# Value differences of a stick-breaking attention spread over a projection and four head pairs, and each pair's output split issued after the next pair's turned weights

## The chip, the cores and the metric

The kernel runs on one core of one Trainium2 chip. A core has TensorE (PE, with its weight loads shown as PEld), VectorE (DVE), ScalarE (ACT), GpSimd (POOL) and SyncE (SP), each with its own queue of instructions that it works off in order. Transfers are requested from a queue (here SP's and GpSimd's) and carried out beside the engines. The metric is the device time of the whole program in microseconds; lower is better. Three runs of the kernel before took 1161.62, 1164.15 and 1165.39 us, the median is 1164.15 us.

## The reference, cut to what matters

The program is a trunk of two layers on a sequence of 512 tokens with 1024 channels in fp32. The change lies in the first token mixer, a stick-breaking attention with 16 heads of 64 channels:

```python
z = einsum('bhtd,bhsd->bhts', q, k) * scale
before = s_idx < t_idx
log_beta = log_sigmoid(z)
log_1m = where(before, log_sigmoid(-z), 0.0)
later = cumsum(log_1m, reverse=True) - log_1m
a = where(before, exp(log_beta + later), 0.0)
out = einsum('bhts,bhsd->bhtd', a, v)
...
y = stick_breaking_mixer(h, w_qkv, w_o)
x = x + gate * rms_norm(y, post_g)
```

What follows (a SwiGLU network, a chunked token-mixing layer, a second SwiGLU) is untouched by the change.

## The kernel before, in words

**Number format.** Every product in fp32 quality is made of three matmuls. An fp32 value is split into a high part in the fast format fp32r and the low rest: `split` (line 112) copies the high part on ScalarE (line 116) and lets VectorE subtract it (recorded at line 69, the helper through which the kernel calls VectorE). Weights are loaded into `raw`, split into `wh` and `wl` (lines 154 to 160) and kept in five buffers; `wget` asks for the weights that come next and prepares up to three tiles beyond.

**The attention without a product of weights.** The tokens are laid out in reverse, so the sum over later positions is a running product. With p the sigmoid of minus the score, a scan on VectorE (`left`) gives the remaining stick after each key. An attention weight is the difference of two neighbouring remainders; so the sum over keys is rewritten as a sum of the remainders times the differences of neighbouring rows of V. These differences are U. `u_steps` (line 629) makes them for one half of V's columns, one token tile of 128 rows at a time: GpSimd's queue requests a copy `vs` of the tile moved by one row (`shifted`, with one row of the next tile), VectorE subtracts the tile from it, and `split` writes U's high and low parts, ScalarE first, then VectorE. There is one buffer `vs`, so the copy for the next tile is requested after the low part of this one. The last tile has no next row; GpSimd clears the last rows first.

**The stages in question.** First V's first half is projected, with the query and key of pair 0 among it. Its four banks are copied to `vf` (line 626). Then, as the program is written, all four U steps of the first half are issued, and then V's second half is projected over eight k steps (line 954), with the scores of pair 0 after k = 1 and k = 4 and a step of a background task, `ada_step`, after each k from 2 on. That task makes three adaLN vectors, G, A and B: one weight load and one product on VectorE per step, at the end a broadcast through two matmuls in the first score bank `z`. 36 steps finish it.

Then `late_u` is set up for the second half's U, and a loop runs over the eight head pairs (line 971). While a pair's weights are turned and multiplied, TensorE also gets "fills": matmuls of the query and key projections (`pqk`) of later pairs, and of the output projection (`y`) towards the end. Pairs 0 to 4 have the same numbers of fills. Within a pair the order is:

- `flip(LATE)` turns the weights of the late key blocks (token tiles 2 and 3) on TensorE into `tw`; ScalarE and VectorE write the high and low part `ar` (lines 905 and 69)
- one U step; fills; scores of the next pair for two key blocks (`B31`); fills and an `ada_step`
- `values(LATE)` multiplies U with `ar` into `av`; one U step; fills
- `flip(EARLY[0])`; one U step; fills; scores for block 2; fills and an `ada_step`
- `values(EARLY[0])`, `flip(EARLY[1])`; one U step; fills; scores for block 0; fills and an `ada_step`
- `values(EARLY[1])`, then `finish`: each bank's crossed half is copied by ScalarE to `of` (line 933), VectorE adds the main half, and `split` makes `o`, the input of the output projection.

The U steps of the loop are used up in pair 0, since there are four. The second half's U is first needed in pair 4.

**What sets the order.** Each engine works in order. On TensorE the order is written out from the first pair's query on (`pe["chain"]`), on VectorE from the loop's setup on (`dve.chain`), for all that is called through the helper; the weights' low parts are called past it. Everything else, ScalarE, GpSimd, SP, and VectorE in V's second half, is ordered by the framework's planner from a model of its own: among the instructions that it believes ready it takes the one that stands first in the program.

**Buffers.** `vf` lies in a pool `npool` of two buffers, which `finish` also takes `of` from. Most other tiles (hT, U, q, k, o, G, A, B) are slots of one pool of 28.

Of the kernel before, what the change touches and what calls it, by code (L numbers as in the profile page):

```python
# [13 lines left out]
P = 128  # L14
# [17 lines left out]
def trunk(ctx: ExitStack, tc: tile.TileContext, A: dict, out: bass.AP):  # L32
# [16 lines left out]
    def nm(s):  # L49
        uid[0] += 1  # L50
        return f"{s}_{uid[0]}"
# [577 lines left out]
    def u_steps(vf, hf, pool):  # L629

        def shifted(tt):
            vs = pool.tile([P, 512], F32, tag="vs", name=nm("vs"))
            if tt == NT - 1:
                nc.gpsimd.memset(vs[96:P, :], 0.0)
            nc.gpsimd.dma_start(out=vs[0 : P - 1, :], in_=vf[tt][1:P, :])
            if tt < NT - 1:
                nc.gpsimd.dma_start(out=vs[P - 1 : P, :], in_=vf[tt + 1][0:1, :])
            return vs

        vs = shifted(0)  # L640
        yield
        for tt in range(NT):
            dve.tensor_tensor(vs[:], vs[:], vf[tt], ALU.subtract)
            src = vs[:].rearrange("p (a e c) -> p a e c", a=4, e=2)
            dst = U[hf][tt][:].rearrange("p a (q c) -> p a q c", q=4)
            split(dst[:, :, 0::3, :], dst[:, :, 1:3, :], src)
            if tt + 1 < NT:
                vs = shifted(tt + 1)
            yield

    onec = oneb[:, 0:1]
# [115 lines left out]
    with tc.tile_pool(name="att", bufs=1) as att, tc.tile_pool(name="att2", bufs=2) as att2:  # L767
# [78 lines left out]
        def attend(i):  # L846

            weights = {}
            vhf = i // 4

            def layout(js):
                offs, N = {}, 0
                for j in js:
                    offs[j] = N
                    N += T - P * j
                return offs, N  # L860

            def scores(js):

                q, kt = qk[i]
                offs, N = layout(js)
                for j in js:
                    o, n = offs[j], T - P * j
                    js_ = slice(j * P, (j + 1) * P)
                    for t, (a, b) in enumerate(((0, 0), (0, 1), (1, 0))):
                        for h in range(2):  # L870
                            hr = slice(64 * h, 64 * h + 64)
                            mm(
                                zb[h][:, o : o + n], q[hr, a, js_], kt[hr, b, j * P : T],
                                j == js[0] and t == 0, t == 2,
                            )
                tri, at, M = gaps[js]
                free = left[js[0] != 2]
                r = free.pop(0)
                free.append(r)
                with tc.issue_after(table.ins):  # L880
                    for h in range(2):
                        for j in js:
                            o, n = at[h, j], T - P * j
                            last_act[0] = act.activation(
                                g[:, o : o + n], zb[h][:, offs[j] : offs[j] + n], AF.Sigmoid, scale=-1.0
                            )
                dve.tensor_tensor_scan(r[:, :M], g[:, :M], tri, 1.0, ALU.mult, ALU.max)
                for h in range(2):
                    for j in js:
                        weights[h, j] = r, at[h, j]  # L890

            turned = {}

            def flip(blocks, h):

                ps = tw[h]
                n = 0
                for jj, js in blocks:
                    for j in js:
                        r, o = weights[h, j]  # L900
                        o += (jj - j) * P
                        transpose(ps[:, n : n + P], r[:, o : o + P])
                        n += P
                ar = att2.tile([P, 2, T], F32R, tag="ar", name=nm("ar"))
                act.activation(ar[:, 0, :n], ps[:, :n], AF.Identity, bias=minus)
                dve.scalar_tensor_tensor(
                    ar[:, 1, :n], ps[:, :n], 1.0, ar[:, 0, :n].bitcast(F32),
                    ALU.subtract, ALU.subtract,
                )
                turned[blocks[0][0], h] = ar  # L910

            def values(blocks, h, stop):

                ar = turned[blocks[0][0], h]
                start = blocks is LATE
                n = 0
                for jj, js in blocks:
                    w = len(js) * P
                    for e in range(2):
                        mm(  # L920
                            av[h][:, js[0] * P : js[0] * P + w],
                            U[vhf][jj][:, i % 4, h * P : (h + 1) * P], ar[:, e, n : n + w],
                            start and n + e == 0, stop and jj == 3 and e == 1,
                        )
                    n += w

            def finish():
                o = slot(F32R, "o")
                o8.append(o)
                f = npool.tile([P, 512], F32, tag="n", name=nm("of"))  # L930
                for h in range(2):
                    main, cross = [slice(64 * e, 64 * e + 64) for e in (h, 1 - h)]
                    act.activation(f[main, :], av[h][cross, :], AF.Copy)
                for h in range(2):
                    main = slice(64 * h, 64 * h + 64)
                    dve.tensor_tensor(f[main, :], av[h][main, :], f[main, :], ALU.add)
                split(o[:, 0, :], o[:, 1, :], f[:])

            return scores, flip, values, finish

        with tc.issue_after(last_sqrt[0].ins):
            table = nc.scalar.preload_act_table_set("sigmoid_and_others")
# [2 lines left out]
        evac_k(0, pk0)  # L945
        LATE = ((2, (2,)), (3, (2, 3)))
        EARLY = ((0, (0,)), (1, (0, 1))), ((2, (0, 1)), (3, (0, 1)))
        for _ in u_steps(vf0, 0, att):
            pass
        vb = [bank("v1") for _ in range(NT)]  # L950
        zb = [bank("z") for _ in range(2)]
        bg0.bank = bg.bank = lambda: zb[0]
# [1 line left out]
        for k in range(KD):  # L954
            if k % 2 == 0:
                wv = wget(("wv", 1, k // 2))
            v_step(vb, 1, k, wv)
            if k in (1, 4):
                cur[0](B31 if k == 1 else B2)
            if k > 1:  # L960
                ada_step()
        late_u = u_steps(v_evac(vb), 1, att)
        next(late_u)
        dve.chain = True
# [4 lines left out]
        for n in FIRST:  # L969
            fill(n, 2)  # L970
        for i in range(NPAIR):
            scores, flip, values, finish = cur
            more = i + 1 < NPAIR
            F = iter(FILLS if i < 5 else LAST[i - 5])
            flip(LATE, 0)
            flip(LATE, 1)
            next(late_u, None)
            fill(next(F))
            if more:
                cur = attend(i + 1)  # L980
# [1 line left out]
            fill(next(F), 1)  # L982
            values(LATE, 0, False)
            values(LATE, 1, False)
            next(late_u, None)
            fill(next(F))
            flip(EARLY[0], 0)
            flip(EARLY[0], 1)
            next(late_u, None)
            fill(next(F))  # L990
            if more:
                cur[0](B2)
# [2 lines left out]
            values(EARLY[0], 1, False)  # L995
            flip(EARLY[1], 0)
            flip(EARLY[1], 1)
            next(late_u, None)
            fill(next(F))
            if more:  # L1000
                cur[0](B0)
            fill(next(F), 1)
            values(EARLY[1], 0, True)
            values(EARLY[1], 1, True)
            finish()
        for _ in fgen:
            pass
        ada_step(99)
# [517 lines left out]
```

## Time and profile before

| | us |
|---|---|
| median of three runs | 1164.15 |
| the profiled execution | 1167.44 |
| its span | 1165.7 |
| TensorE busy | 1127.5 (97%) |
| VectorE busy | 933.7 (80%) |
| ScalarE busy | 596.0 (51%) |

The profiled execution's own time is 1.7 us above its span. A row of the profile names the line, the engine, what is written from what, and how long it took; the brackets at its end give the time for which the engine stood idle ahead of it and the instruction that ended the wait. Because a helper records every call, line 93 is every matmul and line 69 nearly every VectorE instruction; the names of the tiles tell them apart. `clock` or PEclk is the share of TensorE's full clock that was granted.

### The profile page before, as it was taken

The page shows a single profiled execution, that of the slowest core. Times are in us where ns is not written, and L with a number is a line of the kernel's source. Part 1 is how long each engine was busy: PE and PEld are TensorE (multiplying, and loading weights), DVE is VectorE, ACT ScalarE, POOL GpSimd, SP SyncE. Part 2 cuts the span into 40 slices and gives each one's busy share as a digit, 9 for nine tenths or more (in the row PEclk, how much of TensorE's full clock was granted, in tenths as well). Part 3 has the DMA queues.
Part 4 walks back from the last instruction along what each step waited for, and adds up shares of the span by engine and source line. Part 5 has one row for each costly group of instructions (what it writes and reads, how often), then busy time and mean ns, then how long its engine had stood idle before and what let it go on. Part 6 is the DMA issues. An engine that isn't in the chain of part 4 may idle for free.

```text
span 1165.7 us, 18660 instructions
## 1 busy us (share of the span) xinstructions
PE 1127.5 (97%) x7436; PEld 1014.1 (87%) x7436; DVE 933.7 (80%) x1215; ACT 596.0 (51%) x985; POOL 30.0 (3%) x55
## 2 busy tenths in 40 slices
PE   6979889999999999999999999999999999999997
PEld 4757668778899999998887898988999999999996
DVE  4967789975998898879677956668979898789996
ACT  5434455664655555555243543526555555565652
POOL 0021100000000000001000000000000000000000
PEclk9989999999999999999999999999999999999999
DMA  7846425313424444327887475224343343222242
GB/s 298 339 153 205 129 93 160 121 62 118 154 78 140 145 145 143 127 79 268 273 280 245 160 236 179 91 81 160 105 139 132 129 144 126 93 91 91 91 150 104
DMA packets 51644, 176.52 MB, mean 151 GB/s; under 512 B 6106, under 2 KB 9434, under 8 KB 51556
## 3 DMA queue, kind: packets, MB, share of 16 engines
q1 hardware_dynamic: 48996, 166.94, 42.6%
q0 software_dynamic: 2560, 8.39, 1.9%
q8 instruction: 58, 0.95, 0.3%
q14 instruction: 30, 0.25, 0.1%
HBM read 164.82 MB, written 8.39 MB: 149 GB/s over the span
## 4 chain that ended last, share of the span: by engine, by line
PE 71%; DVE 8%; DMA 5%; ACT 2%; issue 1%; DVEq 0%; SPq 0%; ACTq 0%
PE r L93 32%; PE y L93 8%; PE pqk L93 4%; DMA rawada<-in_ada 4%; PE X L93 4%; PE v L93 4%; PE gu L93 4%; PE Y L93 3%; PE u L93 3%; PE av L93 2%; DVE wl L160 1%; PE W L93 1%; PE Z L93 1%; DVE t L69 1%; PE z L93 1%
## 5 line engine op out<-in xcount | busy, mean ns | idle before, releaser
L93 PE MATMUL r<-Sh,wh 128*128 128x256 f32 x608 | 172.1, 283 | 0.0
L93 PE MATMUL r<-Sl,wh 128*128 128x256 f32 x608 | 172.1, 283 | 0.0
L93 PE MATMUL r<-Sh,wl 128*128 128x256 f32 x608 | 172.1, 283 | 0.0
L159 ACT ACTIVATE wh<-raw 128x1024 fp32r<-128x1024 f32 x87 | 91.7, 1057 | 117.3 <-PE y L93 58.9
L93 PE MATMUL y<-wh,as 128*128 128x512 f32 x480 | 150.6, 391 | 0.4 <-DVE G L69 0.4
L116 ACT ACTIVATE wh<-f 128x1024 fp32r<-128x1024 f32 x87 | 92.2, 1060 | 91.8 <-PE r L93 66.5
L69 DVE TENSOR_TENSOR wl<-f,wh 128x1024 fp32r<-128x1024 f32 x87 | 106.1, 1220 | 39.8 <-ACT wh L116 39.7
L160 DVE TENSOR_TENSOR wl<-raw,wh 128x1024 fp32r<-128x1024 f32 x87 | 105.9, 1219 | 36.2 <-ACT wh L159 36.0
L93 PEld LDWEIGHTS r<-Sh,wh 128*128 128x128 f32 x608 | 116.7, 192 | 0.0
L93 PEld LDWEIGHTS r<-Sl,wh 128*128 128x128 f32 x608 | 116.7, 192 | 0.0
L93 PEld LDWEIGHTS r<-Sh,wl 128*128 128x128 f32 x608 | 116.7, 192 | 0.0
L93 PEld LDWEIGHTS y<-wh,as 128*128 128x128 f32 x480 | 90.0, 188 | 19.4 <-DVE G L69 0.9
L93 PE MATMUL y<-wl,as 128*128 128x512 f32 x240 | 93.7, 390 | 0.0
L93 PE MATMUL r<-hTh,wh 128*128 128x256 f32 x304 | 87.7, 292 | 0.0
L93 PE MATMUL r<-hTl,wh 128*128 128x256 f32 x304 | 85.4, 282 | 0.0
L93 PE MATMUL r<-hTh,wl 128*128 128x256 f32 x304 | 81.0, 283 | 0.0
L93 PE MATMUL r<-hTh,b 128*128 128x256 f32 x304 | 61.0, 283 | 0.0
L93 PEld LDWEIGHTS r<-hTh,wh 128*128 128x128 f32 x304 | 58.0, 191 | 2.3 <-DVE gu L69 0.6
L93 PE MATMUL v<-wh,hTh 128*128 128x512 f32 x128 | 52.2, 408 | 7.1 <-ACT wh L159 5.4
L93 PEld LDWEIGHTS r<-hTl,wh 128*128 128x128 f32 x304 | 58.1, 191 | 0.1
L116 ACT ACTIVATE wh<-rawx 128x1024 fp32r<-128x1024 f32 x38 | 40.3, 1060 | 34.6 <-PE r L93 31.8
L93 PEld LDWEIGHTS r<-hTh,wl 128*128 128x128 f32 x304 | 55.9, 191 | 0.0
(268 smaller groups left out, 2984.5 us busy)
## 6 DMA issues: line engine op xcount, KB each, us to landing
rawada<-in_ada SPq DMA_DIRECT2D x80, 512.0 KB, 4.5
rawy<-in_wy SPq DMA_DIRECT2D x38, 512.0 KB, 3.5
rawx<-in_wx SPq DMA_DIRECT2D x38, 512.0 KB, 4.0
raw<-in_wdown SPq DMA_DIRECT2D x22, 512.0 KB, 4.8
raw<-in_wdn SPq DMA_DIRECT2D x22, 512.0 KB, 3.5
raw<-in_wqk SPq DMA_DIRECT2D x16, 512.0 KB, 4.2
ada<-in_ada0p SPq DMA_DIRECT2D x12, 512.0 KB, 7.8
raw<-in_wgu SPq DMA_DIRECT2D x12, 512.0 KB, 3.5
```

The lines of the kernel that those rows point to most:

```text
L69: b = getattr(nc.vector, op)(*args, **kw)
L93: b = nc.tensor.matmul(o, l, r, start=start, stop=stop, skip_group_check=True)
L116: act.activation(hi, src, AF.Copy)
L159: act.activation(h[:], raw[:], AF.Copy)
L160: nc.vector.tensor_tensor(l[:], raw[:], h[:].bitcast(F32), ALU.subtract)
```

## The change

- `u_steps` takes the token tiles in the order 2, 3, 0, 1.
- The four U steps of V's first half are no longer issued as a block ahead of V's second half. The first shifted copy is requested there; the steps follow after k = 1, 3, 5 and 7.
- In V's second half `ada_step` is called after k = 2, 4 and 6 instead of after each k from 2 to 7.
- In the pair loop there is one U step per pair, in pairs 0 to 3, after `flip(EARLY[0])`. In pairs 4 to 7 an additional `ada_step` stands in that place.
- `finish` is cut in two. `gather` copies and adds into `of`, now a slot of the pool of 28. `part` splits `of` into `o`, and is called in the next pair, after its `flip(LATE)`; for the last pair, after the loop.

```diff
-        vs = shifted(0)
+        turns = (2, 3, 0, 1)
+        vs = shifted(turns[0])
         yield
-        for tt in range(NT):
+        for n, tt in enumerate(turns):
             dve.tensor_tensor(vs[:], vs[:], vf[tt], ALU.subtract)
...
             split(dst[:, :, 0::3, :], dst[:, :, 1:3, :], src)
-            if tt + 1 < NT:
-                vs = shifted(tt + 1)
+            if n + 1 < NT:
+                vs = shifted(turns[n + 1])
             yield
...
-            def finish():
-                o = slot(F32R, "o")
-                o8.append(o)
-                f = npool.tile([P, 512], F32, tag="n", name=nm("of"))
+            def gather():
+                f = slot(F32, "of", 1, 512)[:, 0, :]
+                fs.append(f)
                 for h in range(2):
                     main, cross = [slice(64 * e, 64 * e + 64) for e in (h, 1 - h)]
                     act.activation(f[main, :], av[h][cross, :], AF.Copy)
                 for h in range(2):
                     main = slice(64 * h, 64 * h + 64)
                     dve.tensor_tensor(f[main, :], av[h][main, :], f[main, :], ALU.add)
-                split(o[:, 0, :], o[:, 1, :], f[:])
-
-            return scores, flip, values, finish
+
+            def part():
+                o = slot(F32R, "o")
+                o8.append(o)
+                split(o[:, 0, :], o[:, 1, :], fs[0])
+
+            return scores, flip, values, gather, part
...
-        for _ in u_steps(vf0, 0, att):
-            pass
+        early_u = u_steps(vf0, 0, att)
+        next(early_u)
...
-            if k > 1:
+            if k in (2, 4, 6):
                 ada_step()
+            if k % 2:
+                next(early_u)
...
             flip(LATE, 0)
             flip(LATE, 1)
-            next(late_u, None)
+            if i:
+                last_part()
...
             values(LATE, 0, False)
             values(LATE, 1, False)
-            next(late_u, None)
             fill(next(F))
             flip(EARLY[0], 0)
             flip(EARLY[0], 1)
-            next(late_u, None)
+            if i < 4:
+                next(late_u)
+            else:
+                ada_step()
...
             flip(EARLY[1], 0)
             flip(EARLY[1], 1)
-            next(late_u, None)
...
             values(EARLY[1], 0, True)
             values(EARLY[1], 1, True)
-            finish()
+            gather()
+            last_part = part
+        last_part()
```

More of the change, by code (lines that the diff above doesn't have):

```diff
@@ L846, in attend @@
         def attend(i):
-            weights = {}
+            weights, fs = {}, []
             vhf = i // 4
@@ L971, in trunk @@
         for i in range(NPAIR):
-            scores, flip, values, finish = cur
+            scores, flip, values, gather, part = cur
             more = i + 1 < NPAIR
```

## The prediction

> **What bounds the kernel now.** I read the page's head first, then the busy time by stage, then TensorE's instructions in order of time with the idle time in front of each, and last VectorE's and ScalarE's instructions around the waits so found.
>
> ```profile
> span 1165.7 us, 18660 instructions
> PE 1127.5 (97%) x7436; PEld 1014.1 (87%) x7436; DVE 933.7 (80%) x1215; ACT 596.0 (51%) x985; POOL 30.0 (3%) x55
> ```
>
> TensorE has work for 97% of the span, so only TensorE's idle time, or time at a lowered clock, can be won. The change touches the stage from about 71 us to 270 us: V's second half, a stretch of pure projections, and the eight head pairs. I cut it at the first turned weight block of each pair. The columns are busy us (instructions) of TensorE, its weight loads, VectorE, ScalarE and GpSimd, then granted clock, DMA share and GB/s.
>
> ```profile
> core 0: us, PE busy (x) PEld busy (x) DVE busy (x) ACT busy (x) POOL busy (x), PEclk, DMA share, GB/s
> 71.50:81.47 9.97, 1.88 (x15) 1.05 (x14) 8.45 (x9) 4.88 (x9) 1.04 (x2) 0.69 0.09 26
> 81.47:101.40 19.93, 19.93 (x81) 15.79 (x82) 11.24 (x13) 7.00 (x10) 3.58 (x6) 0.90 0.59 189
> 101.40:117.19 15.79, 14.82 (x68) 11.62 (x66) 12.22 (x11) 7.65 (x11) 0.51 (x1) 1.00 0.69 236
> 117.19:138.90 21.71, 19.73 (x118) 15.47 (x116) 15.32 (x20) 10.93 (x21) 4.08 (x7) 1.00 0.40 120
> 138.90:165.29 26.39, 21.64 (x120) 16.85 (x119) 21.61 (x24) 12.47 (x25) 0.00 (x0) 0.94 0.38 123
> 165.29:184.45 19.16, 19.16 (x118) 15.40 (x117) 17.52 (x19) 11.11 (x22) 0.00 (x0) 1.00 0.39 126
> 184.45:203.65 19.20, 19.20 (x119) 15.46 (x118) 17.86 (x20) 10.97 (x22) 0.00 (x0) 1.00 0.44 136
> 203.65:222.79 19.14, 19.14 (x118) 15.43 (x117) 17.83 (x20) 10.91 (x22) 0.00 (x0) 1.00 0.49 164
> 222.79:242.00 19.21, 19.21 (x121) 15.12 (x119) 16.34 (x21) 12.93 (x26) 0.00 (x0) 1.00 0.11 36
> ```
>
> Pairs 0 to 4 carry the same TensorE work (the same list of fills), yet they take 21.71, 26.39, 19.16, 19.20 and 19.14 us. Pairs 2 to 4 leave TensorE no idle time, so 19.15 us is what a pair costs when nothing is late, and pairs 0 and 1 together lose 48.10 - 38.30 = 9.8 us. In pairs 2 to 4 VectorE is busy 17.5 to 17.9 of 19.15 us: it is the second limit, and close. The waits themselves are in TensorE's order of time (start, length, instruction, in brackets the idle time ahead and who ended it):
>
> ```profile
> 77.96 0.79 PE L93 MATMUL v<-wh,hTh 128*128 128x512 f32 x1 [5.37 <-ACT wh L159]
> 81.47 0.79 PE L93 MATMUL v<-wl,hTh 128*128 128x512 f32 x1 [2.71 <-DVE wl L160]
> 104.59 0.96 PE L93 MATMUL z<-k,q 64*128 64x512 f32 x6 [0.97 <-DVE G L69]
> 129.50 1.08 PE L93 MATMUL av<-ar,U 128*128 128x128 f32 x7 [0.25 <-DVE ar L69]
> 137.84 1.22 PE L93 MATMUL av<-ar,U 128*128 128x256 f32 x7 [1.74 <-DVE ar L69]
> 141.84 0.33 PE L93 MATMUL z<-k,q 64*128 64x128 f32 x2 [0.74 <-ACT k L116]
> 142.69 1.02 PE L93 MATMUL z<-k,q 64*128 64x128 f32 x10 [0.51 <-DVE k L69]
> 146.66 0.33 PE L93 MATMUL av<-ar,U 128*128 128x128 f32 x1 [0.68 <-DVE of L69]
> 149.81 1.45 PE L93 MATMUL av<-ar,U 128*128 128x128 f32 x7 [2.83 <-DVE ar L69]
> 246.76 1.08 PE L93 MATMUL av<-ar,U 128*128 128x128 f32 x7 [0.44 <-DVE ar L69]
> 259.06 0.33 PE L93 MATMUL av<-ar,U 128*128 128x128 f32 x1 [0.39 <-ACT ar L905]
> 261.53 1.08 PE L93 MATMUL av<-ar,U 128*128 128x128 f32 x7 [0.73 <-DVE ar L69]
> ```
>
> Three groups: V's second half waits 5.37 + 2.71 = 8.1 us for its second weight tile and then runs at granted clock 0.90, about (1 - 0.90) x 19.93 = 2.0 us more; pairs 0 and 1 wait 0.25 + 1.74 + 0.74 + 0.51 + 0.68 + 2.83 = 6.75 us, the remaining 3.0 of their 9.8 us being mostly the clock (0.94 in pair 1: (1 - 0.94) x 26.39 = 1.6) and small gaps; pairs 6 and 7 wait 0.44 + 0.39 + 0.73 = 1.6 us.
>
> **The change part by part.** *The U steps of V's second half taken out of pair 0.* One such step, and the place where it hurts:
>
> ```profile
> 132.79 0.69 DVE L69 TENSOR_TENSOR vs<-vs,vf 128x512 f32<-128x512 f32 x1 [2.88 <-DMA vs<-vf]
> 133.52 0.63 ACT L116 ACTIVATE U<-vs 128x512 fp32r<-128x512 f32 x1 [1.15 <-DVE vs L69]
> 134.18 0.69 DVE L69 TENSOR_TENSOR U<-vs,U 128x512 fp32r<-128x512 f32 x1 [0.70 <-ACT U L116]
> 137.10 1.28 DVE L69 SCALAR_TENSOR_TENSOR ar<-tw,ar 128x512 fp32r<-128x512 f32 x2
> 148.50 0.68 DVE L69 TENSOR_TENSOR o<-of,o 128x512 fp32r<-128x512 f32 x1
> 149.20 1.02 DVE L69 SCALAR_TENSOR_TENSOR ar<-tw,ar 128x384 fp32r<-128x384 f32 x2
> ```
>
> VectorE's order is written out in this stage, so a step holds it for 0.69 + 0.70 (waiting for ScalarE's high part) + 0.69 = 2.07 us, and the third step held it 2.88 us more because its shifted rows were not there. Four steps are 8.3 us, with that wait 11.2 us, in a pair where VectorE has some 1.3 us to spare. That is why `ar` at 137.10 came 1.74 us late for TensorE, and the lag then shows at `k`, `of` and `ar` of pair 1. After the change pair 0 has one step, and each step's rows are loaded a pair ahead, so the 2.88 us wait goes too: VectorE's chain in pair 0 is shorter by 3 x 2.07 + 2.88 = 9.1 us against a lag of 6.75 us of waits on TensorE. I therefore let the whole 9.8 us go. Bounds: -9.8, and -3.2 if only the waits up to 142.69 (0.25 + 1.74 + 0.74 + 0.51) belong to those steps.
>
> *One step each in pairs 0 to 3, and the split of `o` behind the next pair's `ar`.* Here is a pair without waits:
>
> ```profile
> 184.73 1.26 DVE L69 SCALAR_TENSOR_TENSOR B<-rawada,sc,B 128x1024 f32<-128x1024 f32 x1
> 188.00 0.69 DVE L69 TENSOR_TENSOR o<-of,o 128x512 fp32r<-128x512 f32 x1 [0.70 <-ACT o L116]
> 188.72 1.02 DVE L69 SCALAR_TENSOR_TENSOR ar<-tw,ar 128x384 fp32r<-128x384 f32 x2
> 189.69 1.08 PE L93 MATMUL av<-ar,U 128*128 128x128 f32 x8
> ```
>
> `ar` ends at 189.74, as TensorE begins to use it at 189.69: no slack. `part` takes 0.70 + 0.69 = 1.39 us from in front of `ar`; the 0.70 us disappears, since ScalarE's half of `o` is done while VectorE does the two `ar`. So `ar` gains 1.39 us of slack and the pair 0.70 us of VectorE. Against that stands 2.07 us for the U step: a pair with three adaLN products needs 17.85 + 2.07 = 19.9 us of VectorE for 19.15 us of TensorE, 0.77 us too much in pairs 1 and 3. Pair 2 has two products by the count of steps (no. 23 starts B and multiplies nothing), 1.26 less, and so gives back 0.5 us. The lag after pair 3 is 0.77 - 0.50 + 0.77 = 1.0 us, inside 1.39 us; as pair 0 ends with little in hand, I charge 1.2 us. Bounds: 0 (all inside the slack) and the three steps of pairs 1 to 3 fully on the path, 6.2 us.
>
> *The adaLN steps.* V's half runs 3 instead of 6, so numbers 12 to 14 (G's two halves, and A's first load) move behind it, every later step comes three places later, and pairs 4 to 6 run one more each: 1.26 us of VectorE in pairs 4 and 5, where VectorE then needs 19.1 and about 17.6 us. Cover: no U step there. If the cover fails, 3 x 1.26 = 3.8 us, the upper bound; I take 0. Their loads stay in SP's queue in the same order among the weights, three steps later; nothing waits for A or B before the output projection. G's two products leave V's half and with them the wait at 104.59 (0.97 us); they now run in the 17 fills ahead of pair 0, where they need the score bank between two scores. I take -0.5 us, bounds -1.0 and +1.0.
>
> *The U steps of the first half, behind V's products.* In the text they come after the weights; whether they do on the engines is another matter:
>
> ```profile
> 62.73 2.64 ACT L626 ACTIVATE vf<-v 128x512 f32<-128x512 f32 x4 [3.95 <-PE v L93]
> 63.64 0.67 POOL L635 DMA_DIRECT2D vs<-vf  x1 [2.35 <-ACT vf L626]
> 71.52 0.69 DVE L69 TENSOR_TENSOR vs<-vs,vf 128x512 f32<-128x512 f32 x1 [4.08 <-DMA vs<-vf]
> 75.24 0.63 ACT L116 ACTIVATE acch<-G 128x512 fp32r<-128x512 f32 x1 [2.31 <-DVE G L69]
> 76.83 1.08 ACT L159 ACTIVATE wh<-raw 128x1024 fp32r<-128x1024 f32 x1
> ```
>
> In this stage ScalarE and VectorE are ordered by the planner. It put `acch`, which the program issues after k = 5, ahead of `wh`, which it issues at k = 0; so it takes what it believes ready, not what stands first. The shifted rows are requested at the same place as before, so I expect the planner to place the first U step about as before, and the wait for the weight tile to stay. The step now begins with token tiles 2 and 3, whose copies end two of four later: 2 x 2.64 / 4 = 1.3 us later at GpSimd's queue, an upper bound of +1.3; if the weights do come first, 8.1 + 2.0 = 10.1 us go. I take -0.5, near the stay, since the row of `acch` speaks for it.
>
> *Tail and buffers.* In pairs 6 and 7 the split of `o` no longer stands before `ar`: of the 1.6 us I take -1.0; one more broadcast in pair 6 may cost what was won (bound +0.5). `of` leaves the two-buffer pool for a slot of 28; I count 27 in use at the worst, in pair 3, so no wait. The U order 2, 3, 0, 1 fits the late blocks, used first. GpSimd's one extra duty, clearing rows for tile 3, comes earlier, beside other work.
>
> **Sum.** -9.8 + 1.2 + 0 - 0.5 - 0.5 - 1.0 = -10.6 us. Against the profiled execution, 1167.44 us (its span of 1165.7 and 1.7 around it), that is 1156.8; that execution stands 3.3 us above the median of 1164.15, against which the forecast is 1153.6 us.
>
> **The clock.** The rows show the granted clock at 0.94 in the pair with the 2.83 us wait. [...]
>
> **Rivals.** (1) *V's half is freed too.* The planner puts the weights first; 10.1 instead of 0.5 us: 1144.0. For it: ScalarE stood idle before 71.5 us with nothing but a U step to wait for. Against it: the row of `acch`.
> (2) *Slower: VectorE becomes the bound of the pairs.* Each step's 2.07 us in pairs 1 to 3 and each extra product fall on the path, 6.2 + 3.8 = 10.0 us, and of the first pairs' waits only 3.2 us go: 1164.15 + 6.8 = 1170.9. For it: 17.85 of 19.15 us busy, and `ar` with no slack. Against it: 1.39 us of slack is made at exactly that place. It decides once `ar` comes about 2 us late in each of five pairs (9.8 / 5).
> (3) *The stalls only move.* The lag of pair 0 is made by something else, such as its late second projection `k` at 141.84, and the 9 us of relief ends in idle VectorE: 1163, no change.
> (4) *The clock's fall in pair 1 has another cause than its waits.* Then its 1.6 us stay: 1153.6 + 1.6 = 1155.2. Against it: the clock is 1.00 in the neighbouring pairs, where no wait reaches 2 us.
>
> **Chances.** Forecast 0.55 (own range 1150 to 1158), (1) 0.17, (2) 0.14, (3) 0.11, (4) 0.03. Most likely 1153.6. The range goes from 1143, which takes in (1), to 1165, which takes in (3); (2) is left out. Faster, beyond the 0.3% (3.5 us) that a measurement of this kernel can tell from no change: 0.75; within it 0.11; slower 0.14.
>
> **What would show it.** Right: pairs 0 and 1 each at 19.2 to 20 us with the clock at 1.00; no VectorE wait for shifted rows; `o` split after `ar` with no 0.70 us wait; VectorE 19 us busy or nearly so in pairs 1 and 3, TensorE waits there under 1 us each. Wrong: a pair over 20.5 us; waits before `av` in each pair, which is (2); or the 5.37 us wait gone, which is (1).

## The result, and the profile after

The changed kernel takes 1159.66 us (median of 15 runs, 1155.85 to 1164.11) against 1164.40 us for the kernel before in the same comparison (15 runs, 1161.62 to 1170.49). The ratio is 0.9954, with a 95% interval of 0.9939 to 0.9969: 0.3 to 0.6% faster, some 5.4 us (4.7 by the medians). The forecast was a gain of 10.6 us, so the sign was right and half of the gain did not come.

The head of the page of the changed kernel; the profiled execution took 1160.02 us:

```profile
span 1158.3 us, 18661 instructions
PE 1124.4 (97%) x7436; PEld 1013.5 (88%) x7436; DVE 932.9 (81%) x1215; ACT 596.5 (52%) x985; POOL 30.0 (3%) x55
```

The same work is done; only TensorE's time without work or at a lowered clock can have changed. The busy time by stage, cut as before at the first turned block of a pair: two rows of V's second half, then pairs 0 to 6.

```profile
71.09:81.55 10.46, 1.34 (x7) 0.50 (x5) 7.75 (x8) 4.87 (x9) 1.08 (x2) 0.62 0.08 25
81.55:101.00 19.45, 19.45 (x76) 15.53 (x77) 10.54 (x12) 7.36 (x11) 2.07 (x4) 0.85 0.61 202
116.97:136.11 19.14, 19.14 (x117) 15.43 (x116) 15.07 (x18) 10.16 (x20) 1.05 (x2) 1.00 0.42 132
136.11:155.25 19.14, 19.14 (x118) 15.44 (x117) 18.24 (x22) 11.48 (x23) 1.04 (x2) 1.00 0.46 146
...
193.63:212.83 19.20, 19.20 (x118) 15.43 (x117) 18.02 (x20) 10.90 (x22) 0.00 (x0) 1.00 0.47 155
212.83:232.83 20.00, 17.99 (x111) 13.77 (x109) 18.31 (x22) 10.87 (x23) 0.00 (x0) 1.00 0.43 142
232.83:250.58 17.75, 15.27 (x98) 11.63 (x97) 13.82 (x18) 11.17 (x22) 0.00 (x0) 1.00 0.26 90
```

Pairs 0 and 1 now take 19.14 us each with no idle time on TensorE and the clock at 1.00. Pairs 5 and 6, where the kernel before took these times, are the ones that became longer; before:

```profile
222.63:240.51 17.88, 17.88 (x112) 14.21 (x111) 15.01 (x20) 11.65 (x24) 0.00 (x0) 1.00 0.13 42
240.51:256.44 15.93, 14.87 (x97) 11.30 (x95) 12.85 (x16) 10.55 (x21) 0.00 (x0) 1.00 0.28 100
```

All waits of TensorE in the changed kernel's stage, in order of time:

```profile
77.56 0.80 PE L93 MATMUL v<-wh,hTh 128*128 128x512 f32 x1 [5.92 <-ACT wh L159]
81.55 0.79 PE L93 MATMUL v<-wl,hTh 128*128 128x512 f32 x1 [3.20 <-DVE wl L160]
218.79 1.08 PE L93 MATMUL av<-ar,U 128*128 128x128 f32 x7 [0.92 <-DVE ar L69]
226.73 0.50 PE L93 MATMUL z<-accl,ones 128*128 128x512 f32 x1 [1.08 <-DVE accl L69]
235.40 1.13 PE L93 MATMUL z<-k,q 64*128 64x128 f32 x12 [1.04 <-DVE A L69]
238.43 0.50 PE L93 MATMUL z<-acch,ones 128*128 128x512 f32 x1 [0.31 <-ACT ga L885]
242.80 0.50 PE L93 MATMUL z<-accl,ones 128*128 128x512 f32 x1 [1.12 <-DVE accl L69]
253.21 0.33 PE L93 MATMUL av<-ar,U 128*128 128x128 f32 x1 [0.41 <-ACT ar L906]
```

The six waits of pairs 0 and 1 are gone, and between V's second half and pair 5 none is left. Most of what is new hangs on the adaLN task: `acch` and `accl` are the high and low half of one of its vectors on the way to a product with `ones`, `z` is the score bank that the product is written to, and `A` is the read that frees the bank for the next score.

The same time from point to point, for every kernel of this study, in the one profiled execution of each. "First score" is where V's second half begins (the first product of `z` from `k` and `q`); the next columns run from there to pair 0, and then over the pairs named.

| kernel | first score at | to pair 0 | pairs 0-1 | pairs 2-3 | pairs 4-6 |
|---|---|---|---|---|---|
| before | 71.46 | 45.73 | 47.94 | 38.36 | 52.95 |
| after | 70.50 | 46.47 | 38.28 | 38.38 | 56.95 |
| `a_again` (after) | 68.04 | 46.92 | 38.29 | 38.37 | 57.24 |
| `b_again` (before) | 68.37 | 45.91 | 48.31 | 38.38 | 52.93 |
| `e1_ada_as_before` | 67.12 | 46.87 | 38.26 | 38.36 | 52.26 |
| `e2_late_u_only` | 68.85 | 45.13 | 38.38 | 39.71 | 54.21 |
| `e3_part_only` | 70.64 | 46.77 | 47.10 | 38.26 | 52.24 |
| `e3_again` | 68.04 | 45.67 | 44.51 | 38.27 | 52.26 |
| `e5_extra_step_only` | 70.10 | 46.78 | 38.26 | 38.35 | 53.98 |
| `e6_weights_first` | 66.85 | 37.18 | 38.26 | 38.36 | 52.32 |
| `w1_weights_first_again` | 67.35 | 37.21 | 38.26 | 38.36 | 52.26 |
| `w2_extra_step` | 70.16 | 37.85 | 38.26 | 38.35 | 53.92 |
| `w3_late_and_extra` | 66.78 | 42.16 | 38.28 | 38.38 | 57.02 |
| `w4_late_steps_only` | 70.44 | 42.14 | 38.28 | 38.38 | 55.23 |

In the kernel before, the prediction cut pairs 2 to 5 some 0.15 us later than this table does; its 48.10 us for pairs 0 and 1 are 47.94 here.

Between the two first rows: -0.96 us ahead of the stage, +0.74 up to pair 0, -9.66 in pairs 0 and 1, +0.02, +4.00 in pairs 4 to 6, and -1.54 after pair 7 begins; together -7.40, the difference of the spans (1165.7 and 1158.3). The first column differs by 4.7 us over the executions, and by 3.1, 2.5 and 2.6 us between two executions of one and the same kernel (before, after, `e3_part_only`); so the -0.96 us can't be put down to the change, nor can the -1.54, as is shown under the tail below. That is the reason why 7.4 us here stand beside 5.4 us of the comparison.

### The profile page after: what moved, and what is told of

The parts are those of the page before. It is cut to its first block, busy times and chain, and to the rows that moved or that the text cites. A ratio compares the mean times of both kernels' runs of the same rounds, so it can differ in the third digit from the quotient of the medians.

```text
span 1158.3 us, 18661 instructions
## 1 busy us (share of the span) xinstructions
PE 1124.4 (97%) x7436; PEld 1013.5 (88%) x7436; DVE 932.9 (81%) x1215; ACT 596.5 (52%) x985; POOL 30.0 (3%) x55
## 4 chain that ended last, share of the span: by engine, by line
PE 84%; DMA 6%; DVE 5%; ACT 2%; issue 2%; SPq 0%; POOL 0%; DVEq 0%; ACTq 0%; POOLq 0%
PE r L93 33%; PE y L93 10%; PE v L93 7%; PE pqk L93 6%; PE gu L93 5%; PE u L93 4%; PE X L93 4%; DMA rawada<-in_ada 4%; PE Y L93 3%; PE z L93 2%; PE av L93 2%; PE W L93 1%; PE Z L93 1%; PE tp L101 1%; PE tw L101 1%
```

## The experiments

### Is the loss of pairs 0 and 1 regular? (`b_again`)

The kernel before, unchanged.

> The kernel before, unchanged, profiled a second time, to see what of the 9.8 us that pairs 0 and 1 lose belongs to every execution. If the 2.83 us wait and the fall of the clock behind it are regular: pairs 0 and 1 again take about 48 us and the span is near 1165. If the first profiled execution, 3.3 us above its median, was an unlucky one: the pairs take some 45 to 46 us, with the granted clock at 1.00 in pair 1, and the span is near 1162.

It took 1166.41 us. Pairs 0 and 1 took 48.31 us, with the same chain of waits and the clock at 0.93 in pair 1. So the 9.8 us that the forecast starts from are there in a second execution too, on other events ahead of the stage (first score 3.1 us earlier).

### The adaLN steps put back (`e1_ada_as_before`)

```diff
-            if k in (2, 4, 6):
+            if k > 1:
                 ada_step()
...
             if i < 4:
                 next(late_u)
-            else:
-                ada_step()
```

> The changed kernel with the adaLN steps where they were (six in V's second half, none added in pairs 4 to 7). If the later adaLN steps ate the gain: the waits of pairs 5 and 6 (0.92, 1.08, 1.04, 0.31 and 1.12 us) fall to about 0.5 us, a wait of about 1 us for G returns ahead of pair 0, and the time is 3 to 4 us below the changed kernel's, about 1156. If the lag comes from the U steps of pairs 1 to 3 or from the split of o: pair 5 still waits about 0.9 us before av, and the time stays within 1 us of 1159.7.

1155.20 us (4 runs, 1153.29 to 1156.31), ratio 0.9908 (0.9884 to 0.9931): 10.7 us below the kernel before by the ratio. The interval lies below that of the change (0.9939 to 0.9969). Pairs 5 and 6 of this variant:

```profile
209.79:227.67 17.88, 17.88 (x113) 14.23 (x112) 15.07 (x20) 11.66 (x24) 0.00 (x0) 1.00 0.17 60
227.67:242.87 15.20, 14.59 (x96) 11.28 (x95) 12.61 (x16) 10.52 (x21) 0.00 (x0) 1.00 0.31 104
```

33.08 us, against 37.75 in the changed kernel. Of the five waits none is left in pair 5, and one of 0.52 us in pair 6. So the missing half of the gain lies in the adaLN edit, and all else of the change is worth what was forecast for the whole; that the two figures are so close is chance, as the single terms below differ. One part of the expectation did not come: no wait for G returned ahead of pair 0, though G's two broadcasts are in V's second half again (the last at 98.77 us, the next score at 101.40 without a wait).

### The late U steps alone (`e2_late_u_only`)

The kernel before, with one U step of the loop's four kept per pair (the one after `flip(EARLY[0])`), and `of` in a slot of the pool of 28:

```diff
             flip(LATE, 1)
-            next(late_u, None)
...
             values(LATE, 1, False)
-            next(late_u, None)
...
             flip(EARLY[1], 1)
-            next(late_u, None)
```

> The kernel before with one U step of V's second half per pair in pairs 0 to 3 and nothing else, but that the value sums lie in the large pool, since the small one is held by V until pair 3. If the four U steps made the lag of pairs 0 and 1: both take 19.2 to 20 us, about 9 us come back. If the place of the split of o is as important: pairs 1 to 3 wait 0.5 to 1 us each before av, since VectorE then needs 17.9 + 2.07 us with 0.70 us of waiting for o in it, and 6 to 7 us come back.

1156.53 us (4 runs, 1155.27 to 1159.83), ratio 0.9925 (0.9900 to 0.9951). Pairs 0 and 1 take 38.38 us: this edit alone frees them, and 8.7 us come back. The slot for `of` is not what does it, since the next variant has it too and keeps most of the loss. But pairs 3 and 4 now wait for the turned weights:

```profile
178.27 1.08 PE L93 MATMUL av<-ar,U 128*128 128x128 f32 x7 [0.99 <-DVE ar L69]
198.69 1.09 PE L93 MATMUL av<-ar,U 128*128 128x128 f32 x7 [1.04 <-DVE ar L69]
```

Pairs 2 and 3 lose 39.71 - 38.36 = 1.35 us, pairs 4 to 6 54.21 - 52.95 = 1.26 us. The U step of a later pair is not free by itself: the waits of the second case came, in two pairs instead of three.

### The split of `o` moved alone (`e3_part_only`, `e3_again`)

The kernel before, with `finish` cut into `gather` and `part` and `part` called behind the next pair's `flip(LATE)`, as in the change; the U and adaLN steps as before.

> The kernel before with the split of o behind the next pair's turned weights and nothing else. If the U steps made the lag: pair 0 still waits 1.7 us before av, and of the 2.83 us in pair 1 only 1.4 us go, so 2 to 4 us come back. If the split of o made it: pairs 0 and 1 lose less than 4 us together, and 6 us or more come back.

1159.45 us (10 runs, 1156.26 to 1164.68), ratio 0.9943 (0.9928 to 0.9958). Pairs 4 to 6 take 52.24 us, 0.71 less than before. Pairs 0 and 1 take 47.10 us and so keep most of their loss, and the profiled execution was the slowest of its ten, so it was profiled once more:

> The kernel before with only the split of o moved, profiled a second time: its first profiled execution was the slowest of its ten. If the fall of the clock in pair 1 comes in some executions and not in others: pair 1 now takes about 21.5 us with the clock at 1.00, against 24.7 us, with the same waits. If it always comes: 24.7 us again.

Now 1158.47 us, and 44.51 us for pairs 0 and 1. The stretch from pair 0's last wait to the second block of pair 1, with TensorE's wait ahead of it; first in the first execution:

```profile
138.41 1.60 PE L93 MATMUL av<-ar,U 128*128 128x256 f32 x7 [2.06 <-DVE ar L69]
```

```profile
138.41:153.00 14.59, 12.60 (x54) 10.06 (x55) 12.71 (x14) 6.63 (x13) 0.00 (x0) 0.77 0.45 134
```

and then in the second:

```profile
134.37 1.22 PE L93 MATMUL av<-ar,U 128*128 128x256 f32 x7 [1.70 <-DVE ar L69]
```

```profile
134.37:146.56 12.19, 9.53 (x54) 7.29 (x55) 11.16 (x14) 6.50 (x13) 0.00 (x0) 1.00 0.44 134
```

The same 54 matmul records are 9.53 instead of 12.60 us busy where the clock did not fall, and the stretch is 2.4 us shorter. The waits ahead of it and in it are much alike: 2.06, 0.32, 0.68 and 0.99 us in the one, 1.70, 0.47, 0.52, 0.69 and 0.99 in the other. On such a chain of short waits the clock fell in the one execution and not in the other. The traces show what went with it. In the kernel before, the clock stands at 0.50 from 75.24 to 85.48 us and from 150.33 to 153.74, in the changed kernel from 73.63 to 87.28: that is 3, 1 and 4 times 3.41 us, and the two falls of the kernel before are 22 times 3.41 us apart. So time is cut here into windows of that length, counted from a change of the clock. Here are the two windows of the first execution behind which it fell, and then, of those that hold the waits of the second, the window in which TensorE did least:

```profile
135.64:139.05 3.41, 1.35 (x9) 0.94 (x7) 3.41 (x5) 1.11 (x3) 1.92 (x3) 1.00 0.40 92
145.88:149.29 3.41, 1.74 (x8) 1.04 (x7) 3.35 (x6) 2.92 (x7) 0.00 (x0) 1.00 0.29 71
```

```profile
140.32:143.73 3.41, 2.25 (x10) 1.43 (x8) 3.35 (x5) 2.25 (x6) 0.00 (x0) 1.00 0.17 24
```

In the second execution nearly the same waits are shared out over three windows (2.53, 2.43 and 2.25 us busy), and the clock stays. In the kernel before, the window that holds the 2.83 us wait has 0.58 us of work (146.92 to 150.33 us); the clock fell behind that wait in both executions (0.94 and 0.93 in pair 1).

By the times this move alone wins 6.6 us, more than the 2 to 4 us of the first case and about as much as the whole change, though pairs 0 and 1 still lose 8.8 and 6.2 of their 9.7 us. Pairs 0 to 6 together are 1.65 and 4.21 us shorter than before in the two executions; what the rest comes from is open.

### What in the adaLN edit costs? (`a_again`, `e5_extra_step_only`)

> The changed kernel, unchanged, beside the next ones on the same chip. If the profiled execution already seen is typical: pairs 0 to 4 at 19.1 to 19.2 us, waits of 4 to 5 us in pairs 5 to 7, a time 4.5 to 6.5 us below the kernel before. If most executions differ from it: other waits in pairs 1 to 4.

1158.66 us (9 runs), ratio 0.9937 (0.9915 to 0.9960), an interval that overlaps the one of `e1_ada_as_before` a little. By the medians that is 7.0 us below the kernel before, somewhat more than expected. Pairs 4 to 6 took 57.24 us, and the waits are those listed above to a few hundredths. The execution shown is typical.

`e5_extra_step_only` is the changed kernel with six steps in V's second half again, and the added step of pairs 4 to 7 kept (the first hunk of `e1_ada_as_before` alone).

> The changed kernel with six adaLN steps in V's second half again, but the added step of pairs 4 to 7 kept. If the added step costs, because it shortens the way from the split of a vector to its product: pairs 4 and 5 wait some 1 to 2.5 us, and the time is that much above the variant with the adaLN steps as before (ratio 0.9908). If only the delay by three steps costs: the waits of pairs 5 and 6 are gone, and the ratio is 0.991.

1157.75 us (7 runs), ratio 0.9933 (0.9911 to 0.9955). By the times alone it can't be told from the changed kernel. In the stage, pairs 4 to 6 take 53.98 us, 1.72 more than in `e1_ada_as_before`, which is the first case; pairs 4 and 5:

```profile
193.49:213.20 19.71, 19.71 (x120) 15.80 (x119) 19.51 (x21) 11.55 (x23) 0.00 (x0) 1.00 0.55 173
213.20:232.99 19.79, 18.31 (x112) 14.30 (x111) 14.65 (x20) 11.97 (x25) 0.00 (x0) 1.00 0.12 42
```

```profile
222.92 0.48 PE L93 MATMUL z<-acch,ones 128*128 128x512 f32 x1 [1.45 <-DVE A L69]
225.11 0.69 DVE L69 TENSOR_TENSOR accl<-B,acch 128x512 fp32r<-128x512 f32 x1 [0.80 <-PE pqk L93]
```

The one large new wait of this variant is for the score bank: the product of B's first half can't be written until VectorE has read A's second half from it (`A`). That half is written by 218.52 us, but the read begins at 222.09, since it stands in VectorE's order behind a scan of 2.3 us and two low parts (of a weight tile and of a query). In `e1_ada_as_before` the same read begins at 222.09 too, 0.03 us after the half is written (222.06). By the row of pair 5, 14.65 of 19.79 us, VectorE seems to have time, but the row of pair 4 has it busy for 19.51 of 19.71 us, and it has no gap over 0.14 us from 187.26 to 224.31. Its idle time in pair 5 begins behind the wait, with the 0.80 us of the last row.

### The weights first, and the two halves of the adaLN edit apart (`e6_weights_first`, `w1` to `w4`)

The changed kernel's V half still waits 5.92 + 3.20 us. The next variant is `e1_ada_as_before`, with the planner told to place the scores, the adaLN and the U steps of V's second half behind the two instructions that split the second weight tile. The work is the same.

```diff
-            act.activation(h[:], raw[:], AF.Copy)
-            nc.vector.tensor_tensor(l[:], raw[:], h[:].bitcast(F32), ALU.subtract)
+            hi = act.activation(h[:], raw[:], AF.Copy)
+            lo = nc.vector.tensor_tensor(l[:], raw[:], h[:].bitcast(F32), ALU.subtract)
+            made[key] = hi, lo
...
+            hi, lo = made["wv", 1, 1]
+            with tc.issue_after(hi.ins), tc.issue_after(lo.ins):
                 if k in (1, 4):
                     cur[0](B31 if k == 1 else B2)
                 if k > 1:
                     ada_step()
                 if k % 2:
                     next(early_u)
```

> The variant with the adaLN steps as before, and in V's second half the scores, the U steps and the adaLN steps held behind the split of the second weight tile, on ScalarE and VectorE. If the planner's order makes the wait there (the weights have long landed): the 6.2 and 3.2 us go, the clock stays at 1.00, and the time falls by 8 to 11 us more, to a ratio near 0.982. If the weights really come late, or the tail of the stage is bound by transfers: the wait stays near 5 us or comes back later in the stage, and less than 4 us are won.

1144.86 us (4 runs, 1144.54 to 1145.41), ratio 0.9829 (0.9808 to 0.9850): the fastest of all, 1.2% below the changed kernel (`a_again`) and 1.7% below the kernel before. V's second half by stage, up to the first fill and from there to pair 0, and its one larger wait:

```profile
66.85:88.57 21.72, 20.03 (x95) 15.36 (x95) 18.30 (x19) 10.01 (x17) 3.07 (x5) 1.00 0.55 176
88.57:104.03 15.46, 14.84 (x67) 11.63 (x66) 13.29 (x14) 8.64 (x13) 2.07 (x4) 1.00 0.67 202
```

```profile
87.73 0.47 PE L93 MATMUL z<-acch,ones 128*128 128x512 f32 x1 [1.55 <-ACT U L116]
```

The same work up to the first fill took, in `e1_ada_as_before`:

```profile
67.12:99.23 32.11, 22.76 (x96) 17.69 (x96) 21.00 (x23) 13.70 (x22) 4.09 (x7) 0.79 0.44 140
```

32.11 became 21.72 us. Of the 10.4 us, 2.7 are the clock (22.76 against 20.03 us busy for the same matmuls), the rest idle time; 0.7 us come back in the next stretch (15.46 against 46.87 - 32.11 = 14.76), so 9.7 us stay. The transfers were no limit in this stretch: they go through at 176 GB/s where it was 140. The tile's load is requested 8.8 us ahead of the first score in this variant and in the changed kernel alike (61.66 and 70.50 us in the latter), and ScalarE's split of it, in this variant, is

```profile
62.33 1.06 ACT L160 ACTIVATE wh<-raw 128x1024 fp32r<-128x1024 f32 x1 [0.22 <-DMA raw<-in_wv]
```

So the weights have landed 4.5 us ahead of the first score (66.85 us); in the changed kernel the same split comes 5.9 us behind it (76.43 and 70.50 us). The wait for the weights was made by the order of instructions on ScalarE and VectorE, and the first case of the expectation came. Which of the three that are held back (scores, U steps, adaLN steps) made how much of it was not tried apart.

On this base, w1 to w4 were run together on one chip, to tell the two halves of the adaLN edit apart without the disturbed V half ahead. (Three steps in V's half with no added step anywhere is not among them; `w4_late_steps_only` adds a step in pairs 6 and 7 alone.)

> The variant with the second weight tile first, again, as the base of the next three on the same chip. If its small spread is its own: all its runs within 1 us, near 1145 us.

1146.45 us (4 runs, 1142.92 to 1150.15), ratio 0.9831 (0.9803 to 0.9859). The small spread was chance.

`w2_extra_step`: the base with the added step (`else: ada_step()`) in pairs 4 to 7.

> The base with the added adaLN step of pairs 4 to 7. If the added step costs in itself, as the stage of the profiled execution had it without the hold (pairs 4 to 6 took 53.98 us against 52.26): 1.7 us above the base. If the costs seen there came of the disturbed V half ahead: no more than 0.5 us above it.

1148.20 us, ratio 0.9847 (0.9830 to 0.9864), 1.75 us above w1 by the medians with overlapping intervals, and 53.92 against 52.26 us in pairs 4 to 6: +1.66 us, the first case.

`w4_late_steps_only`: the base with

```diff
-                if k > 1:
+                if k in (2, 4, 6):
                     ada_step()
...
             if i < 4:
                 next(late_u)
+            elif i > 5:
+                ada_step()
```

> The base with three adaLN steps in V's second half, and the added step in pairs 6 and 7 alone, so that the task comes to its end in pair 6. If the delay costs in itself, through products that wait for their loads and vectors that are split late: pairs 4 and 5 still lose 2 to 3 us. If it is the number of steps in a pair that costs: pairs 4 and 5 take 19.2 and about 18 us as in the base, and the loss of 1 to 2 us lies in pair 6, where three broadcast steps meet.

1155.08 us (4 runs, 1151.99 to 1157.57), ratio 0.9896 (0.9871 to 0.9921), 8.6 us above w1; 2.97 us of it lie in pairs 4 to 6, and most of the rest ahead of pair 0 (see `w3_late_and_extra`). Pairs 5 and 6, and the largest wait in them:

```profile
208.44:224.86 16.42, 16.42 (x106) 13.16 (x105) 14.91 (x18) 9.72 (x21) 0.00 (x0) 1.00 0.45 145
224.86:244.47 19.61, 16.66 (x103) 12.39 (x101) 16.66 (x21) 12.37 (x23) 0.00 (x0) 1.00 0.30 107
```

```profile
234.85 0.48 PE L93 MATMUL z<-acch,ones 128*128 128x512 f32 x1 [1.45 <-DVE A L69]
```

The delay costs nothing in pairs 4 and 5 (pair 4 takes 19.20 us; pair 5 is even 1.46 us shorter than the 17.88 of `e1_ada_as_before`, since its steps are now products on VectorE alone). The price falls in pair 6, 19.61 against 15.20 us, where the broadcasts meet that used to be spread over two pairs: pairs 4 to 6 together +2.97 us. That is the second expectation as to the place; the size was forecast at 1 to 2 us.

`w3_late_and_extra`: the changed kernel with the weights first and nothing else.

> The changed kernel with the second weight tile first and nothing else: three adaLN steps in V's second half and the added step in pairs 4 to 7. If the adaLN term of the changed kernel is what its pairs 4 to 6 show (56.95 us against 52.26): 4.7 us above the base. If a part of it came of the disturbed V half ahead: less than 3 us above it.

1154.41 us (4 runs), ratio 0.9900 (0.9872 to 0.9928): 8.0 us above w1, more than either theory. In pairs 4 to 6 it is 57.02 - 52.26 = 4.76 us, as forecast, and 1.66 + 2.97 = 4.63, so the two halves of the edit add up. Beside it stands a new wait ahead of pair 0, which w4 has too (42.16 and 42.14 us up to pair 0 against 37.21); with its 4.95 us the profiled executions differ by more than the medians do. TensorE's two rows, and ScalarE's rows between them:

```profile
87.20 0.97 PE L93 MATMUL z<-k,q 64*128 64x512 f32 x6
96.98 0.80 PE L93 MATMUL z<-acch,ones 128*128 128x512 f32 x1 [6.55 <-ACT ga L887]
```

```profile
91.89 1.06 ACT L155 ACTIVATE wh<-raw 128x1024 fp32r<-128x1024 f32 x1 [2.27 <-DMA raw<-in_wqk]
...
94.84 0.63 ACT L116 ACTIVATE U<-vs 128x512 fp32r<-128x512 f32 x1 [0.92 <-DVE vs L69]
...
96.33 1.09 ACT L887 ACTIVATE ga<-z 128x512 f32<-128x512 f32 x2
```

The last score of pair 0 stands in the bank from 88.2 us on, but ScalarE reads it (`ga`) only at 96.33, behind a weight tile whose load has not landed and a U step that VectorE has not yet subtracted. With three steps in V's half, G's broadcast comes behind that score and has to wait for the bank; with six steps it comes ahead of it, and 1.55 us are waited (the row of `e6_weights_first` above). In the changed kernel itself, with its own order in V's half, this wait does not occur.

## Why the prediction was right or wrong

**The U steps out of pair 0 (-9.8): right.** Pairs 0 and 1 went from 47.94 to 38.28 us, -9.66, and `e2_late_u_only` shows that this edit does it alone. So the waits at `k`, `of` and `ar` in pair 1 were the lag of pair 0, and rival (3), a cause elsewhere, is out. Rival (4) did not come: with the waits the fall of the clock went, and pairs 0 and 1 have it at 1.00. In the kernel before, the falls at 75.24 and 150.33 us are 22 windows of 3.41 us apart, and the clock fell behind windows in which TensorE was still at work, for 0.76 and 0.58 us there and for 1.35 and 1.74 us in `e3_part_only`.

**One U step a pair, and the split of `o` behind `ar` (+1.2): the mechanism right, the size too large.** Pairs 2 and 3 went from 38.36 to 38.38 us: 0 instead of 1.2. The slack of 1.39 us is what pays: without the moved split the same steps cost 1.35 + 1.26 = 2.6 us (`e2_late_u_only`), with it nothing (`e1_ada_as_before`). On VectorE, `o` now ends behind `ar` with no wait, and the step's middle 0.70 us is still there:

```profile
178.17 1.02 DVE L69 SCALAR_TENSOR_TENSOR ar<-tw,ar 128x384 fp32r<-128x384 f32 x2
179.11 0.68 DVE L69 TENSOR_TENSOR o<-of,o 128x512 fp32r<-128x512 f32 x1
...
187.37 0.69 DVE L69 TENSOR_TENSOR U<-vs,U 128x512 fp32r<-128x512 f32 x1 [0.70 <-ACT U L116]
```

**The adaLN steps (0): this is the step that failed.** The prediction charged them by VectorE's busy time (1.26 us a product) and put them at nothing, naming as cover that pairs 4 to 6 have no U step. They cost 4.7 us: 56.95 against 52.26 us in pairs 4 to 6. The cover was not there: with the adaLN steps as before, VectorE is busy for 18.98 of the 19.18 us of pair 4 (`e1_ada_as_before`), and the prediction itself had 19.1 of 19.15 us after the change. VectorE's rows in the changed kernel:

```profile
209.24 1.28 DVE L69 SCALAR_TENSOR_TENSOR B<-rawada,sc,B 128x1024 f32<-128x1024 f32 x1 [0.98 <-DMA rawada<-in_ada]
...
218.18 1.02 DVE L69 SCALAR_TENSOR_TENSOR ar<-tw,ar 128x384 fp32r<-128x384 f32 x2
...
226.00 0.68 DVE L69 TENSOR_TENSOR accl<-A,acch 128x512 fp32r<-128x512 f32 x1
```

The added product's weights have not landed when VectorE reaches it (0.98 us). From there, 209.24 us, to 229.00 it works with no gap over 0.14 us, and both waits of pair 5 fall into that time: `ar` begins at 218.18, when TensorE has already run out of work at 217.87 (218.79 - 0.92), and `accl` ends at 226.68 where TensorE has the first half of the broadcast done at 225.65. The two larger waits of pair 6, for `A` and `accl`, fall into a second such stretch, from 231.78 to 243.68 us; there the read that frees the score bank and the low half of B each stand in VectorE's order behind a scan of 2.3 us. The means over the pairs, 18.31 of 20.00 and 13.82 of 17.75 us, hide this. So in pair 5, and at least in part in pair 6, it is rival (2)'s mechanism, VectorE as the bound and late `ar`, in two pairs instead of five.

Rival (2) had priced the steps at 3.8 us, nearer than the forecast's 0, and still too low, since three products are not all that moves. Two causes add up, as w2 and w4 show: the added step in itself 1.66 us, and the delay by three steps 2.97 us (the broadcasts meet in pair 6, where TensorE has only 14.59 us of work in `e1_ada_as_before` against 17.88 in pair 5). How much of each is VectorE's load, and how much the order in which the halves go through the one score bank, no run separates.

**V's second half and the stretch ahead of pair 0 (-0.5 and -0.5): the order right, the sum wrong by 1.7 us.** The planner kept the U step and `acch` ahead of the weight tile, as forecast, and rival (1) did not come. The wait at G ahead of pair 0 is gone, as forecast, but not for the reason given: it is gone in `e1_ada_as_before` too, which keeps G's products in V's half. And the stretch became 0.74 us longer (45.13 to 46.77 us over the five executions with the U steps as before there, 46.47 to 46.92 over the four with the new ones, `e6` and w1 to w4 left out). The rows of ScalarE, VectorE and GpSimd:

```profile
74.84 0.63 ACT L116 ACTIVATE acch<-G 128x512 fp32r<-128x512 f32 x1 [2.32 <-DVE G L69]
76.43 1.08 ACT L159 ACTIVATE wh<-raw 128x1024 fp32r<-128x1024 f32 x1
```

```profile
71.12 0.69 DVE L69 TENSOR_TENSOR vs<-vs,vf 128x512 f32<-128x512 f32 x1 [4.63 <-DMA vs<-vf]
...
77.48 0.69 DVE L69 TENSOR_TENSOR vs<-vs,vf 128x512 f32<-128x512 f32 x1 [2.68 <-DMA vs<-vf]
...
80.30 1.20 DVE L160 TENSOR_TENSOR wl<-raw,wh 128x1024 fp32r<-128x1024 f32 x1
```

```profile
74.53 0.56 POOL L635 DMA_DIRECT2D vs<-vf  x1 [0.30 <-POOL vs L634]
```

The first step's subtraction comes 0.62 us behind the first score (71.12 - 70.50), before it was 0.06 (71.52 - 71.46), and the second step's rows are waited for 2.68 us, before for 0.81: the two waits of TensorE grew by 0.55 + 0.49 = 1.04 us, inside the bound of +1.3 that was given for the new order of the token tiles. What the prediction left out is that the second step is now tile 3, whose last rows GpSimd clears ahead of the copy: the copy is requested 0.93 us behind the first step's end (74.53 - 73.60), before 0.30 (74.31 - 74.01). That duty was said to come beside other work. No run tries it apart. `e6_weights_first` settles what rival (1) had priced: with the weights truly first 9.7 us go, against 10.1 in the prediction.

**Tail (-1.0): about right, at -0.7.** With the adaLN steps as before, pairs 4 to 6 win 52.95 - 52.26 = 0.69 us, and `e3_part_only` shows that the moved split does it (0.71). The prediction's list of those waits leaves out one of 0.53 us at 245.52, for the score bank; it stays (0.52 in `e1_ada_as_before`). What lies behind pair 7's beginning is 1.54 us shorter in the changed kernel (907.72 against 909.26 us), but it lies between 907.5 and 911.3 us over the 14 executions with no pattern by kernel, so nothing is read from it.

**The sum.** Against the forecast's terms, the adaLN steps came out 4.7 us higher, V's half 1.7, the tail 0.3, the U steps out of pair 0 by 0.1, and the later U steps 1.2 us lower: 5.6 us. That makes the stage's gain 10.6 - 5.6 = 5.0 us; the stage itself shows 4.9, the comparison 5.4 by the ratio and 4.7 by the medians. So close a fit is partly luck, since the spread of single executions is several us.

## What to carry to other kernels

A step that is moved into a fully written-out order is to be priced by how late it makes the next link that another engine waits for, and not by the mean load of its engine: VectorE is idle for a fifth of pair 6 (busy 13.82 of 17.75 us), and yet each of its late results there comes out of a stretch in which it works without a gap. Where a tile is awaited although its data have long landed, look at what the planner put ahead of its split on ScalarE and VectorE; a hold behind two instructions won 9.7 us, nearly twice what the whole change did. And one bundled edit can hide a loss in a gain: leaving out the adaLN part doubles the result (10.7 against 5.4 us).

## What the runs showed of the hardware that was not expected

The granted clock fell on waits that are all short: 0.77 over 14.59 us with no wait above 2.06 us in one execution (`e3_part_only`), and 1.00 over the same instructions with nearly the same waits in another (`e3_again`). What it went with is the work of TensorE within windows of 3.41 us. From 40 us on, the clock fell in the kernel before behind windows at full clock with 0.76, 0.58 and 1.27 us of work (the last as the program ends), in the changed kernel behind one with 1.41 us (70.22 to 73.63 us) and an empty one at the end, and in the stretch shown of `e3_part_only` behind 1.35 and 1.74 us. The least work in a window at full clock behind which it did not fall was 2.17 us in the kernel before (140.09 to 143.51 us), 2.29 us in the changed kernel (240.88 to 244.30 us) and, among the windows that hold the waits shown of `e3_again`, 2.25 us. The windows lay differently against the chain of waits in the two executions of one kernel: one ends 0.64 us behind the 2.06 us wait in `e3_part_only` (139.05 and 138.41 us), and 2.54 us behind the 1.70 us wait in `e3_again` (136.91 and 134.37 us). Ahead of 40 us it also fell behind windows with more work, 2.34 us in the kernel before (34.28 to 37.69 us) and 2.58 us in the changed one (32.67 to 36.08 us); so no single bound fits all of these.

And the moment at which the stage begins lies between 66.78 and 71.46 us over 14 profiled executions, and up to 3.1 us apart for one and the same kernel; that is more than half of what the change itself is worth, so only comparisons over many runs, or times from point to point within one execution, show an edit of this size.
